# Letting a second group of heads start its recurrence halfway through the first

## The chip, the cores and the metric

The kernel runs on one core of a Trainium2 chip. The metric is the device time of one execution in microseconds (us), lower being better. Three runs of the kernel before took 1333.76, 1340.32 and 1342.75 us; the median is 1340.32 us. Five engines work side by side, each through its own list of instructions in order: PE (matrix products, with its weight loads shown apart as PEld), DVE (element-wise vector work), ACT (activations and copies), POOL (a second, slower vector engine) and SP (which here only issues DMA transfers). ACT issues DMA transfers too.

## The reference

A trunk of two layers on 512 tokens with 1024 features, in float32. Layer 0 is a spatial-gating MLP and layer 1 an RWKV-7 mixer; each is followed by a gated convolutional feed-forward block, and a last norm closes. The change lies in the RWKV-7 mixer. Its heart is a recurrence over time in 16 heads of 64 features:

```python
def step(state, inp):
    r_t, w_t, k_t, v_t, a_t, b_t = inp
    sa = jnp.einsum('bhvk,bhk->bhv', state, a_t)
    state = (state * w_t[:, :, None, :]
             + sa[..., None] * b_t[:, :, None, :]
             + v_t[..., None] * k_t[:, :, None, :])
    y_t = jnp.einsum('bhvk,bhk->bhv', state, r_t)
    return state, y_t
...
y = wkv7_scan(r_h, decay, k_h, v_h, -kk, kk * a_h)
...
y = (y + bonus.reshape(B, S, D)).astype(h.dtype)
return (y * g) @ w_o
```

Here `r`, `k` and `v` are dense projections of the token-shifted input, `g` is a low-rank gate, and the result `y` is normalised in each head before it is gated and multiplied by `w_o`.

## The kernel before

**The recurrence in chunks.** The 512 steps are cut into eight chunks of 64. Inside a chunk the recurrence is solved with products of 64x64 blocks; from chunk to chunk only the state goes on. What a chunk needs is prepared for all chunks beforehand and kept in DRAM: `std` (the factors that meet the state), `lpd` (lower-triangular blocks, one of which has to be inverted), `btd` and `vtd`. The heads are in pairs (eight pairs, 128 partitions each), and the pairs in two groups of four: group 0 is pairs 0 to 3, group 1 is pairs 4 to 7.

**The stages of the mixer.** `pairs()` makes, pair after pair, what goes to DRAM. `invert(g)` inverts the triangular blocks of group g by substitution: it reads them back (`li`, `lm`, lines L898 and L900), does 31 steps of two DVE instructions each (L910, L911), two transposes (L918, L919), then 32x32 products on PE (L930) with copies on ACT (L932), and stores the result (L915, L935). `scan(g)` is the recurrence of one group. `finish(g, b, y)` normalises the outputs of two chunks, and after every fourth chunk gates them. `projections()` makes keys and values with 128x512 dense products and is used as filler; it ends with the values of the last pairs. `project()` is the product with `w_o`, a filler as well, and may use a group's half only once that group is finished (`gated`).

**One chunk of the scan** is a chain of three links, each ending in a `yield`: the state meets the chunk's factors (PE L978 and L982) and DVE copies the product (L980); the inverted block is applied (PE L991), and DVE and ACT copy the halves (L992, L993); the new state is formed (PE L998, DVE L1001), while PE L1003 makes the chunk's output, which ACT copies (L1006). POOL scales the state meanwhile (L987). The transfers of chunk c+1, six on SP (L954 to L960: `st`, two `vu`, two `pt`, `cbt`), are issued at the start of chunk c.

**What sets the order.** The program is written by Python generators that take turns: `weave(main, side, fill, rate, lag, side_rate)` runs one step of `main`, then `side_rate` steps of `side` and `rate` steps of `fill`; the numbers stand in `RATES`. Around the change the order is:

```python
inv = invert(1)
next(inv)
gw = [gate_weights(g) for g in range(2)]
s0, s1 = scan(0), scan(1)
self.weave(s0, inv, fill, *RATES[2], ktiles=STEPS[2])
...
for k in range(KT):
    nc.sync.dma_start(self.h[k], r.hd[k])
fill = project()
self.weave(s1, None, fill, *RATES[3], ktiles=STEPS[3])
```

A scheduler then places the instructions in each engine's list. In the lists each DMA, from SP or from ACT, takes one of eight counters in turn and waits until the DMA that had this counter before has landed. So a transfer on SP can wait for one that ACT has not issued yet.

Of the kernel before, what the change touches and what calls it, by code (L numbers as in the profile page):

```python
# [2 lines left out]

# [18 lines left out]
KT = 8  # L22
# [7 lines left out]

RATES = ((1.9, 2), (1.9, 6, 2.2), (0.8, 2, 2), (0.6, 2))
WB = 4
FIRST0, WAIT, STEPS = 1, 4, (2, 2, 2, 2)
NKEY = 4
# [105 lines left out]
class Emit:  # L140
# [515 lines left out]
    def rwkv_main(self, r, ctx, gain):  # L656
        nc, tc, A = self.nc, self.tc, self.A
# [21 lines left out]
        ks, used, done, vdone = {}, set(), set(), set()  # L679
# [205 lines left out]

        def invert(g):

# [17 lines left out]
            for j in range(31):  # L905
                ni, nj = 31 - j, j + 1
                a = li[:, j, j + 1:32].unsqueeze(1).to_broadcast([P, nj, ni])
                b = tt[:, 0:nj, j].unsqueeze(2).to_broadcast([P, nj, ni])
                q = pr[:, 0:ni * nj].rearrange("p (c i) -> p c i", i=ni)
                V.tensor_tensor(q, a, b, ALU.mult)  # L910
                V.tensor_tensor(tt[:, 0:nj, j + 1:32], tt[:, 0:nj, j + 1:32], q, ALU.add)  # L911
                if j % 2 == 1:
                    yield
# [34 lines left out]
        chunks, outs, gated = {}, {}, set()  # L948
# [14 lines left out]
        def scan(g):  # L963
            ih = [(i, hd) for i in range(4) for hd in range(2)]
            y, late = None, iter(())
            for c in range(NCH):
                last = c == NCH - 1
                if c == 0:
                    load(g, 0)
# [44 lines left out]
        def finish(g, b, y):  # L1014
# [18 lines left out]
            if b % 2 == 1:  # L1033
                hs = slice((b - 1) * P, (b + 1) * P)
                yield
                if b == 1:
                    outs[g] = [tuple(self.xr.tile([P, T], F32R, tag=t, bufs=10, name=self.uid(t)) for t in ("mxh", "mxl"))
                               for _ in range(4)]
# [35 lines left out]
        def take(gen, n):  # L1074
            for _ in range(n):
                if next(gen, self) is self:
                    return
                yield

        def until(gen, end):  # L1080
            for _ in gen:
                yield
                if end():
                    return


        fill = projections()
# [11 lines left out]
        ep = ctx.enter_context(tc.tile_pool(name="scan", bufs=1))  # L1099
        inv = invert(1)  # L1100
        next(inv)
        gw = [gate_weights(g) for g in range(2)]
        s0, s1 = scan(0), scan(1)
        self.weave(s0, inv, fill, *RATES[2], ktiles=STEPS[2])
        for _ in inv:
# [5 lines left out]
        fill = project()  # L1111
        self.weave(s1, None, fill, *RATES[3], ktiles=STEPS[3])
        for _ in fill:
# [71 lines left out]
```

## Time and profile before

The profiled execution took 1336.87 us, 1335.0 us of which are its span.

| | us |
|---|---|
| median of 3 runs | 1340.32 |
| profiled execution, device time | 1336.87 |
| span of its profile | 1335.0 |
| PE busy in the span | 1269.7 |
| DVE busy | 842.3 |
| ACT busy | 605.6 |
| POOL busy | 140.8 |

The times in this text are counted from the span's start. The first feed-forward block and the mixer's low-rank part and projections lie ahead of 764 us; from there to 956 us lie the two scans, the rest of the fillers and the product with `w_o`; the second feed-forward block fills the rest. PE is counted busy while matmuls are under way, whose ends are modelled; a matmul that runs at half the clock is counted as busy for longer. In a list of instructions in order of time the columns are start, duration, engine, line, operation, output and inputs, count, and in brackets how long the engine was idle before it and what released it.

### The profile page before, as it was taken

Reading aid. Unit: us, or ns where it says so; the run is one execution under the profiler, and the core shown is the slowest. Engines: PE = TensorE matmul, PEld = TensorE weight load, DVE = VectorE, ACT = ScalarE, POOL = GpSimd, SP = SyncE. Lnnn points to the kernel's source line nnn. Section 1 sums busy time; section 2 is a strip of 40 time slices with the busy share of each in tenths; the row PEclk is TensorE's granted clock in tenths of the full one; section 3 lists DMA queues with packets and bytes.
Section 4 is the critical chain, followed back from the end, with each engine's and each line's share of the span. In section 5 each row is a group of like instructions: output and inputs, shape, how many; then the busy total and the mean of one; then the engine's idle time right before and its main releaser. Section 6 shows DMA issues by size and latency. Waiting matters only on the chain.

```text
span 1335.0 us, 19041 instructions
## 1 busy us (share of the span) xinstructions
PE 1269.7 (95%) x7490; PEld 1022.9 (77%) x7490; DVE 842.3 (63%) x1349; ACT 605.6 (45%) x1060; POOL 140.8 (11%) x152
## 2 busy tenths in 40 slices
PE   8999999999999999999989848798999999999996
PEld 6778888888888888777766636676888888888886
DVE  5565477777773335957979476556577777772223
ACT  5444354544443333667875424222454545452221
POOL 3100200000000001311210003232300000000001
PEclk9999999999999999999989869899999999999998
DMA  7232333323333333235866796962223333332322
GB/s 260 82 110 79 95 95 95 95 95 97 101 99 103 118 103 99 83 114 128 199 153 171 160 202 151 242 177 79 79 95 95 95 96 99 103 93 87 103 88 75
DMA packets 135786, 156.63 MB, mean 117 GB/s; under 512 B 64976, under 2 KB 100944, under 8 KB 135696
## 3 DMA queue, kind: packets, MB, share of 16 engines
q10 hardware_dynamic: 30688, 101.07, 24.9%
q1 hardware_dynamic: 105008, 54.34, 16.9%
q8 instruction: 59, 0.97, 0.3%
q14 instruction: 31, 0.25, 0.1%
HBM read 130.74 MB, written 24.64 MB: 116 GB/s over the span
## 4 chain that ended last, share of the span: by engine, by line
PE 79%; DVE 8%; ACT 2%; DMA 2%; issue 2%; POOL 1%; SPq 0%; ACTq 0%; DVEq 0%; POOLq 0%
PE mm L244 8%; PE mm L245 8%; PE mm L246 8%; PE e L244 5%; PE e L246 5%; PE e L245 5%; PE us L244 5%; PE us L246 5%; PE us L245 5%; PE aux L244 5%; PE aux L246 5%; PE aux L245 5%; DVE pr L910 1%; DVE tt L911 1%; PE us L978 1%
## 5 line engine op out<-in xcount | busy, mean ns | idle before, releaser
L205 ACT CAST wh<-w 128x512 fp32r<-128x512 f32 (+1 forms) x393 | 239.3, 613 | 441.5 <-PE mm L245 121.0
L206 DVE TENSOR_TENSOR wl<-w,wh 128x512 fp32r<-128x512 f32 (+1 forms) x385 | 267.0, 696 | 206.0 <-ACT wh L205 200.7
L244 PE MATMUL mm<-mxh,wh 128*128 128x512 f32 x424 | 175.1, 413 | 2.7 <-DVE rt L754 2.0
L245 PE MATMUL mm<-mxl,wh 128*128 128x512 f32 x424 | 169.8, 400 | 0.3 <-DVE mxl L1051 0.3
L246 PE MATMUL mm<-mxh,wl 128*128 128x512 f32 x424 | 168.3, 397 | 1.4 <-DVE wl L206 1.4
L271 POOL TENSOR_TENSOR ss<-ss,sq 128x512 f32<-128x512 f32 x30 | 40.4, 1347 | 777.5 <-issue 594.7
L244 PEld LDWEIGHTS mm<-mxh,wh 128*128 128x128 f32 x424 | 80.7, 191 | 25.3 <-issue 4.5
L246 PEld LDWEIGHTS mm<-mxh,wl 128*128 128x128 f32 x424 | 80.5, 190 | 19.2 <-DVE wl L206 2.1
L245 PEld LDWEIGHTS mm<-mxl,wh 128*128 128x128 f32 x424 | 80.7, 190 | 17.7 <-issue 1.4
L465 ACT ACTIVATE cv<-z,par 128x512 f32<-128x512 f32 x88 | 71.7, 817 | 30.4 <-DVE z L463 30.4
L244 PE MATMUL us<-mxh,wh 128*128 128x512 f32 (+1 forms) x216 | 84.5, 391 | 0.1
L244 PE MATMUL e<-mxh,wh 128*128 128x512 f32 x216 | 84.5, 391 | 0.0
L246 PE MATMUL us<-mxh,wl 128*128 128x512 f32 (+1 forms) x216 | 84.1, 389 | 0.0
L245 PE MATMUL us<-mxl,wh 128*128 128x512 f32 (+1 forms) x216 | 84.1, 389 | 0.0
L245 PE MATMUL e<-mxl,wh 128*128 128x512 f32 x216 | 84.0, 389 | 0.0
L246 PE MATMUL e<-mxh,wl 128*128 128x512 f32 x216 | 84.0, 389 | 0.0
L466 DVE SCALAR_TENSOR_TENSOR cv<-z,par,cv 128x512 f32<-128x512 f32 x88 | 66.0, 752 | 24.3 <-ACT cv L465 24.3
L244 PE MATMUL aux<-mxh,wh 128*128 128x512 f32 x208 | 81.2, 391 | 0.1
L246 PE MATMUL aux<-mxh,wl 128*128 128x512 f32 x208 | 81.1, 390 | 0.0
L245 PE MATMUL aux<-mxl,wh 128*128 128x512 f32 x208 | 80.9, 389 | 0.0
L467 DVE SCALAR_TENSOR_TENSOR cv<-z,par,cv 128x512 f32<-128x512 f32 x88 | 66.0, 752 | 2.9
L244 PEld LDWEIGHTS e<-mxh,wh 128*128 128x128 f32 x216 | 40.6, 188 | 8.8 <-issue 0.5
(1062 smaller groups left out, 2499.0 us busy)
## 6 DMA issues: line engine op xcount, KB each, us to landing
w<-in_wup ACTq DMA_DIRECT2D x88, 512.0 KB, 3.6
w<-in_wdn ACTq DMA_DIRECT2D x32, 512.0 KB, 3.6
st<-std SPq DMA_DIRECT2D x16, 512.0 KB, 6.4
w<-in_wdn ACTq DMA_DIRECT2D x16, 384.0 KB, 3.1
w<-in_wsu ACTq DMA_DIRECT2D x8, 512.0 KB, 3.9
w<-in_wso ACTq DMA_DIRECT2D x8, 512.0 KB, 3.6
w<-in_wk ACTq DMA_DIRECT2D x8, 512.0 KB, 4.3
std<-ar SPq DMA_DIRECT2D x16, 256.0 KB, 4.6
```

What stands on the lines that cost most here:

```text
L205: nc.scalar.copy(hi[r, :n], src)
L206: (lo_eng or nc.vector).tensor_tensor(lo[r, :n], src, hi[r, :n].bitcast(F32), ALU.subtract)
L244: mm(acc, wh, xh, start=first, stop=False)
L245: mm(acc, wh, xl, start=False, stop=False)
L246: mm(acc, wl, xh, start=False, stop=last)
L271: nc.gpsimd.tensor_tensor(self.ss, self.ss, self.sq, ALU.add)
L465: nc.scalar.activation(c, z[:, 2:], AF.Identity, scale=cw(2, i), bias=self.p("conv_b", l * 44 + i))
L466: nc.vector.scalar_tensor_tensor(c, z[:, 1:T + 1], cw(1, i), c, ALU.mult, ALU.add)
L467: nc.vector.scalar_tensor_tensor(c, z[:, 0:T], cw(0, i), c, ALU.mult, ALU.add)
L910: V.tensor_tensor(q, a, b, ALU.mult)
L911: V.tensor_tensor(tt[:, 0:nj, j + 1:32], tt[:, 0:nj, j + 1:32], q, ALU.add)
L978: nc.tensor.matmul(us[H[hd], 0, i, :], st[:, i, hd, 0:C], vu[:, i, hd, :], start=True, stop=True)
```

## The change

- The transfers of group 0's first chunk are issued ahead of those that `invert(1)` starts with.
- Three steps of the filler are put right behind these (`PREFILL`).
- The weights of the gates are fetched and split at the end of the filler, where before they were ahead of the scan.
- `invert(1)` gives way after every step of the substitution where it did after every second one, and gets 3.6 steps for each step of the scan where it got 2.
- After 12 steps (`LEAD`, four chunks) the first weave ends, and what is left of `invert(1)` and of the filler is written out. Then `turns(s0, s1)` alternates one step of group 0 with one of group 1. When group 0 is at its end, group 1 goes on alone.
- The filler's rates are 1.7 for 1.9 in the stage of the pairs, 1.8 for 0.8 in the first four chunks, 0.4 while the groups alternate, and 1 for 0.6 in the rest of group 1.

```diff
-RATES = ((1.9, 2), (1.9, 6, 2.2), (0.8, 2, 2), (0.6, 2))
+RATES = ((1.9, 2), (1.7, 6, 2.2), (1.8, 2, 3.6), (0.4, 2), (1, 2))
...
-        def invert(g):
+        def invert(g, every=2):
...
-                if j % 2 == 1:
+                if j % every == every - 1:
                     yield
...
-                if c == 0:
+                if c == 0 and (g, 0) not in chunks:
                     load(g, 0)
...
+        def turns(a, b):
+            for _ in a:
+                yield
+                if next(b, self) is not self:
+                    yield
...
-        inv = invert(1)
+        load(0, 0)
+        inv = invert(1, 1)
         next(inv)
-        gw = [gate_weights(g) for g in range(2)]
+        for _ in take(fill, PREFILL):
+            pass
+        gw = []
+
+        def gates():
+            for g in range(2):
+                with ExitStack() as after:
+                    for eng in (mybir.EngineType.DVE, mybir.EngineType.Activation):
+                        after.enter_context(tc.issue_after(self.last(eng)))
+                    gw.append(gate_weights(g))
+                yield
+
+        fill = chain(fill, gates())
         s0, s1 = scan(0), scan(1)
-        self.weave(s0, inv, fill, *RATES[2], ktiles=STEPS[2])
+        self.weave(take(s0, LEAD), inv, fill, *RATES[2], ktiles=STEPS[2])
...
         fill = project()
-        self.weave(s1, None, fill, *RATES[3], ktiles=STEPS[3])
+        self.weave(turns(s0, s1), None, fill, *RATES[3], ktiles=STEPS[3])
+        self.weave(s1, None, fill, *RATES[4], ktiles=STEPS[4])
```

No matmul is added or removed; what moves is their order. Lines of the changed kernel are higher by 1 up to the middle of `finish`, then by 2 and more.

SP's list at the end of the pairs, before (`lpd_4080` is group 0's block, `lpd_4081` group 1's; `st`, `vu`, `pt` and `cbt` are a chunk's transfers):

```order
L935 DMA lpd_4080<-lm_5797 32x32x32 x2
L744 DMA vtd<-vt_6589 128x8x64
L898 DMA li_6623<-lpd_4081 64x32x32 x2
L900 DMA lm_6624<-lpd_4081 32x32x32 x2
L954 DMA st_6655<-std 128x1024
L956 DMA vu_6658<-vtd 64x4x64
L957 DMA pt_6656<-lpd_4080 64x4x128
```

The same place now:

```order
L936 DMA lpd_4080<-lm_5797 32x32x32 x2
L955 DMA st_6594<-std 128x1024
L957 DMA vu_6597<-vtd 64x4x64
L958 DMA pt_6595<-lpd_4080 64x4x128
L957 DMA vu_6597<-vtd 64x4x64
L958 DMA pt_6595<-lpd_4080 64x4x128
L961 DMA cbt_6596<-btd 128x512
L899 DMA li_6606<-lpd_4081 64x32x32 x2
L901 DMA lm_6607<-lpd_4081 32x32x32 x2
```

The six transfers of group 0's chunk 0 went ahead of the four with which the substitution of group 1 begins; a store of values (`vtd`) that stood between moved elsewhere.

DVE's list where the substitution meets the scan, before: `wt_6688` is the first copy of chunk 0, and the 17th of the 31 substitution steps (`pr`, `tt`) surrounds it.

```order
L911 TENSOR_TENSOR tt_6625<-tt_6625,pr_6626 128x16x16
L910 TENSOR_TENSOR pr_6626<-li_6623,tt_6625 128x255
L980 COPY wt_6688<-us_6678 128x256
L911 TENSOR_TENSOR tt_6625<-tt_6625,pr_6626 128x17x15
L910 TENSOR_TENSOR pr_6626<-li_6623,tt_6625 128x252
```

The same step of the substitution now; `wt_6812` is the first copy of chunk 1.

```order
L912 TENSOR_TENSOR tt_6608<-tt_6608,pr_6609 128x16x16
L911 TENSOR_TENSOR pr_6609<-li_6606,tt_6608 128x255
L912 TENSOR_TENSOR tt_6608<-tt_6608,pr_6609 128x17x15
L981 COPY wt_6812<-us_6802 128x256
L911 TENSOR_TENSOR pr_6609<-li_6606,tt_6608 128x252
```

The whole of chunk 0 now stands ahead of the substitution's first step, and chunk 1 behind its 17th.

PE's list around chunk 4 of group 0 (`st_7013`), before; L246 is the end of a dense product, L738 and L752 belong to the values:

```order
L246 MATMUL mm_6960<-mxh_5659,wl_6759 128x512
L978 MATMUL us_7259<-vu_7016,st_7013 64x64 x8
L982 MATMUL e_7260<-vu_7016,st_7013 64x64 x8
L738 MATMUL mm_7287<-cst,v_7284 128x128 x4
L991 MATMUL us_7259<-wt_7269,pt_7014 64x64 x8
L752 MATMUL mm_7315<-rt_4089,wb_7313 128x512
L1003 MATMUL e_7260<-vu_7016,pt_7014 64x64
L998 MATMUL us_7259<-vu_7016,cbt_7015 64x64 x8
```

PE's list around the same chunk now (`st_7048` is chunk 4 of group 0, `st_7311` chunk 0 of group 1, `st_7278`'s partner `st_7275` chunk 5 of group 0):

```order
L931 MATMUL aux_7211<-li_7096,lm_6607 32x32 x32
L979 MATMUL us_7286<-vu_7051,st_7048 64x64 x8
L983 MATMUL e_7287<-vu_7051,st_7048 64x64 x8
L992 MATMUL us_7286<-wt_7296,pt_7049 64x64 x8
L1004 MATMUL e_7287<-vu_7051,pt_7049 64x64
L999 MATMUL us_7286<-vu_7051,cbt_7050 64x64 x8
L1004 MATMUL e_7287<-vu_7051,pt_7049 64x64 x7
L979 MATMUL us_7334<-vu_7314,st_7311 64x64
L983 MATMUL e_7335<-vu_7314,st_7311 64x64
L979 MATMUL us_7434<-vu_7278,st_7275 64x64 x8
```

The dense products ahead of chunk 4 and the values' products between its links are gone from this place, since the filler is used up earlier; PE goes from chunk 4 to the first product of group 1, and then to chunk 5 of group 0.

More of the change, by code (lines that the diff above doesn't have):

```diff
@@ L2 @@
 from contextlib import ExitStack
+from itertools import chain
 import numpy as np
@@ L29 @@
 C1 = -0.5 * math.exp(-0.5)
-RATES = ((1.9, 2), (1.9, 6, 2.2), (0.8, 2, 2), (0.6, 2))
+RATES = ((1.9, 2), (1.7, 6, 2.2), (1.8, 2, 3.6), (0.4, 2), (1, 2))
 WB = 4
-FIRST0, WAIT, STEPS = 1, 4, (2, 2, 2, 2)
+FIRST0, WAIT, PREFILL, LEAD, STEPS = 1, 4, 3, 12, (2, 2, 2, 2, 2)
 NKEY = 4
@@ L1036, in finish @@
                 if b == 1:
+                    assert KT - 1 in vdone
                     outs[g] = [tuple(self.xr.tile([P, T], F32R, tag=t, bufs=10, name=self.uid(t)) for t in ("mxh", "mxl"))
```

## Prediction

> **What bounds the kernel now.** I read the page first, then a table by stage, then the instructions of PE, SP and DVE in order of time from 764 to 956 us.
>
> ```profile
> PE 1269.7 (95%) x7490; PEld 1022.9 (77%) x7490; DVE 842.3 (63%) x1349; ACT 605.6 (45%) x1060; POOL 140.8 (11%) x152
> ```
>
> PE is the bound on average, so only time in which PE stands still or runs slowly can be won. The table by stage (length, then the busy time of PE, PEld, DVE, ACT, POOL, the granted clock, and the DMA engines' share and rate) says where that is:
>
> ```profile
> 764.00:784.00 20.00, 1.42 (x7) 0.77 (x6) 11.75 (x29) 6.45 (x11) 2.06 (x4) 0.62 1.07 220
> 784.00:827.00 43.00, 38.48 (x651) 29.38 (x651) 31.96 (x70) 15.86 (x35) 7.01 (x8) 0.90 0.66 152
> 827.00:864.00 37.00, 25.22 (x357) 21.30 (x356) 18.46 (x43) 10.62 (x27) 12.27 (x14) 0.82 1.02 236
> 864.00:921.00 57.00, 57.00 (x738) 41.59 (x737) 32.00 (x71) 16.14 (x39) 17.42 (x18) 1.00 0.59 155
> 921.00:956.00 35.00, 30.93 (x137) 24.85 (x136) 23.71 (x36) 16.64 (x31) 13.74 (x14) 0.95 0.20 61
> ```
>
> PE is idle for 18.6, 4.5, 11.8, 0 and 4.1 us in these five: 39 us of 192. The rows of PE that carry the argument:
>
> ```profile
> 783.66 0.37 PE L978 MATMUL us<-vu,st 128*64 128x64 f32 x2 [18.58 <-DMA vu<-vtd]
> 791.71 0.63 PE L244 MATMUL mm<-mxh,wh 128*128 128x512 f32 x1
> 792.13 0.63 PE L245 MATMUL mm<-mxl,wh 128*128 128x512 f32 x1
> 826.86 0.69 PE L978 MATMUL us<-vu,st 128*64 128x64 f32 x16
> 835.59 0.44 PE L978 MATMUL us<-vu,st 128*64 128x64 f32 x2 [3.14 <-DMA vu<-vtd]
> 844.96 0.33 PE L978 MATMUL us<-vu,st 128*64 128x64 f32 x2 [1.22 <-DVE vu L1001]
> 849.59 0.33 PE L978 MATMUL us<-vu,st 128*64 128x64 f32 x2
> 864.36 0.34 PE L978 MATMUL us<-vu,st 128*64 128x64 f32 x2
> 870.98 0.33 PE L978 MATMUL us<-vu,st 128*64 128x64 f32 x2
> 920.07 0.68 PE L1003 MATMUL e<-vu,pt 64*64 64x64 f32 x14
> 954.80 0.39 PE L245 MATMUL mm<-mxl,wh 128*128 128x512 f32 x1
> 955.03 0.39 PE L246 MATMUL mm<-mxh,wl 128*128 128x512 f32 x1
> ```
>
> Group 0 starts at 783.7 after a wait for its first transfers; its chunk 4 starts at 826.9, 5 at 835.6, 6 at 845.0, 7 at 849.6. Group 1 starts at 864.4, its last chunk ends at 920.7, and the dense products of its half are done at about 955.5. A dense product comes every 0.23 us at full clock (954.80 to 955.03) and every 0.42 at half clock, still eight us after the long gap (791.71 to 792.13).
>
> **The first transfers and the substitution.** SP's rows and two of DVE:
>
> ```profile
> 764.49 1.76 SPq L935 DMA_DIRECT2D lpd<-lm  x2
> 767.53 3.19 SPq L898 DMA_DIRECT2D li<-lpd  x2
> 770.81 3.86 SPq L900 DMA_DIRECT2D lm<-lpd  x2
> 774.84 2.82 SPq L954 DMA_DIRECT2D st<-std  x1
> 778.99 0.62 SPq L956 DMA_DIRECT2D vu<-vtd  x1
> 767.15 0.62 ACT L217 CAST gw<-w 32x512 fp32r<-32x512 f32 x1 [0.58 <-DMA btd<-bt]
> 776.70 0.19 DVE L910 TENSOR_TENSOR pr<-li,tt 128x31 f32<-128x31 f32 x1 [0.24 <-DMA li<-lpd]
> 789.17 0.42 DVE L980 COPY wt<-us 128x256 f32<-128x256 f32 x1
> 797.01 0.42 DVE L980 COPY wt<-us 128x256 f32<-128x256 f32 x1 [0.47 <-PE us L978]
> ```
>
> Now `li` and `lm` go first (767.5 to 774.7) and chunk 0 comes behind. With the order turned, `st` can go when the last pair's stores have landed, as the first `gw` did: 767.2. The second `vu` follows after `st` (0.5), `vu` (0.6) and `pt`, which waits for the block stored at 764.5 (I let it land by 769, an estimate of some 4 us from the two landing times quoted further below): issue at 769.8, and with the 5.5 us that it takes today (778.99 to 784.5) chunk 0 starts at about 774.5, **9 us sooner**. Of the stall of 18.6 us some 13 are covered or gone: 21 dense products more stand ahead of chunk 0 (33 where 12 were), at 0.23 each 4.8 us.
>
> The other side: `li` goes at 771.8 in place of 767.5, is usable 9.2 us later (767.53 to 776.70), and in DVE's list the substitution now stands behind the whole of chunk 0, which, at half clock with five dense products in between, takes from 774.5 to about 783.6. Its first step moves from 776.7 to some 784.3. Seventeen steps take 12.5 us (776.70 to 789.17), with one value's product 13.2: chunk 1's first copy comes at **797.5**, against 797.0 now. The 9 us are gone by then.
>
> **Up to chunk 4.** Today 37.7 us lie between the 17th step (789.2) and chunk 4 (826.9), with chunk 0's 7.8 (789.17 to 797.01) in it. Now chunk 0 is over: 29.9, so chunk 4 could start at 827.4. Three things speak for later: the gates' weights (four DVE instructions, two of 0.7 and two of up to 1.1: 3.5 us) come among DVE's steps here, where today they ran in the stall; ACT's casts of them stand ahead of its copies for chunk 2 and wait for their transfers; and its casts for `w_o` stand ahead of the copy for chunk 3.
>
> ```profile
> w<-in_g ACTq DMA_DIRECT2D x2, 256.0 KB, 3.4
> pt<-lpd SPq DMA_DIRECT2D x32, 128.0 KB, 5.6
> ```
>
> Two waits of 3.4 us, partly under DVE's steps: I take 4 us in all, chunk 4 at **831** (bounds 827, nothing of it, and 838, all of 3.5 and 6.8). Dense work is no cover any more here: 30 dense products are left where 48 were, and they are through during the substitution.
>
> **The hole before group 1.** Today the block's store, the seven reloads of `h` and the chunks' transfers run like this:
>
> ```profile
> 825.97 2.08 SPq L935 DMA_DIRECT2D lpd<-lm  x2
> 836.12 0.53 SPq L954 DMA_DIRECT2D st<-std  x1
> 840.22 0.38 SPq L954 DMA_DIRECT2D st<-std  x1
> 845.71 5.91 SPq L1110 DMA_DIRECT2D h<-hd  x7
> 851.71 0.38 SPq L954 DMA_DIRECT2D st<-std  x1
> 855.50 0.38 SPq L954 DMA_DIRECT2D st<-std  x1
> ```
>
> A chunk's six transfers take 4.1 and 3.8 us to issue. In the changed list the store (2.1, at 830.6, when ACT has copied the last of the blocks), `h` (5.9), chunk 5 of group 0 (4) and chunk 0 of group 1 follow each other; the first `vu` of the latter is issued at about 843 and lands 5 us later: both groups go on at **848**. Chunk 4 runs from 831 to 836 (4.6 from 844.96 to 849.59, without filler), so PE has a new hole of 12 us, with nothing to fill it.
>
> **Taking turns.** Eleven chunks remain: three of group 0, eight of group 1. The first two together I put at 9 us, as chunk 5 took today (835.59 to 844.96, at half clock behind a gap and with gate products). The next six have neither filler nor, most, gate products: between 4.6 (today without filler) and 6.6 (with, 864.36 to 870.98) I take 5.0, near the first, since their links fit between each other's and their transfers come at about 4 to 5 (1.18 MB each by the shapes in SP's list above, at the 236 GB/s of the third stage 5.0). That is 30, to 887. The last three carry two gatings and the filler again and are put at today's (920.7-864.4)/8 = 7.0 each: group 1 ends at **908**, 13 us before 920.7.
>
> **The end.** Today 110 dense products are left at group 1's end, now 150: 40 x 0.23 = 9.2 us more. Of today's 34.8 us PE is idle for 4.1 while the last norm runs, and at half clock behind it; now 30 products stand in that place. I take 6 off: 38 us, so the mixer ends at **946** where it ended at 955.5.
>
> **Sum:** -9.5 us. The second block is unchanged behind it. 1336.9 - 9.5 = 1327.4 against the profiled execution, which was 3.4 below the median: against the median 1330.8. I say 1330.
>
> **A rule of the skill against it.** After the gap of 18.6 us PE still worked at half clock eight us into its work, and there it had dense products. The turns have none, and a hole ahead of them. The Trainium skill, "TensorE: Matmul & The Clock Gate", Part 1 on the clock gate, says that an idle window of about 3.4 us halves the clock and about as much sustained work gives it back; its section on oscillation shows kernels whose waits keep it halved. By this the turns could run at half clock throughout (rival 2).
>
> **The rivals.**
>
> 1. *More is won (0.30).* The waits on ACT before chunk 4 are hidden: chunk 4 at 827, both groups on at 844; the six chunks at 4.6: 844 + 9 + 27.6 + 21 = 901.6, and 37 behind it, 938.6: -17, **1323** by the median. For it: DVE has steps to run meanwhile. Against: it is in order, and ACT too.
> 2. *Half clock through the turns (0.13).* Rows of the same products at the two clocks:
>
> ```profile
> 838.12 1.12 PE L1029 MATMUL aux<-cst,y 128*128 128x128 f32 x4
> 851.32 0.66 PE L1029 MATMUL aux<-cst,y 128*128 128x128 f32 x4
> 839.16 1.12 PE L991 MATMUL us<-wt,pt 64*64 64x64 f32 x16
> 851.90 0.68 PE L991 MATMUL us<-wt,pt 64*64 64x64 f32 x16
> ```
>
>    0.44 us more for one link's products, 1.2 to 1.3 for the three of a chunk; times the six: 7.5, so -2: **1338**. Against it: from 844.96 to 853 today PE ran such chunks at full clock without filler. It decides when gaps of 3 us and more stand between the links.
> 3. *The transfers on SP stop (0.10).* Today SP stood twice for transfers of `w_o` that ACT issues late:
>
> ```profile
> SPq L957 <- DMA w<-in_wo: 12.5, 2, 10.9
> ```
>
>    Each SP transfer waits for the one eight before it, and now also for buffers that two groups share. One stop of 10.9 before group 1 begins and another in the turns, uncovered since no filler is there: +21.8 - 9.5 = +12.3, **1353, slower**. In the list no transfer of ACT stands among those of the turns, which speaks against the second; four stand before chunk 4's end. It decides from 10 us of stops on.
> 4. *Nothing is interleaved (0.05).* Group 1's data come so late that group 0 ends alone: chunks 5 to 7 at 4.6 behind 846, then eight of 7.0 behind 860: 916, with 38: 954, **1339**.
>
> **The numbers.** The forecast has 0.42; its own range, from chunk 4 between 827 and 834 and the six chunks between 4.6 and 6, is 1324 to 1340. The range must also hold rival 1 with the hole smaller by some 5 us (transfers landing sooner) and half of rival 3: 1313 to 1347. One per cent is 13.4 us, about what three runs that differ by 9 can tell. Faster by more: rival 1 and a fifth of the forecast, 0.38. Slower by more: rival 3 lies at that bound, and most of it is counted, 0.08. Within: 0.54.
>
> **What would show it.** Right: chunk 0 at about 774.5 and a substitution beginning near 784; chunk 1's copy at 797; a PE gap of some 12 us between chunk 4 and group 1's first product, ended by a transfer; chunks every 5 us behind it; the last chunk of group 1 near 908. Wrong: a substitution that starts before 780, chunk 4 before 826 or behind 838, a clock of 0.5 through the turns, or SP waiting for `w_o` there.

## The result and the profile after

The kernel after took 1351.02 us in the median of eight runs (1344.6 to 1356.57), the kernel before on the same chip 1339.58 us (eight runs, 1333.76 to 1343.64). The ratio is 1.0085, with a 95% interval of 1.0057 to 1.0114: 11.4 us slower. The prediction had 1330, a range of 1313 to 1347, and 0.08 for slower by over 1%. Direction and range were wrong. That the change stays within 1% had 0.54, but for a gain; that it came out within 1% on the other side is luck and bears out no step.

The profiled execution took 1352.91 us with a span of 1351.1; that of before had 1336.87 and 1335.0. So these two traces differ by 16 us, and the sums below are made against the 16.

The page's line of engine totals, after:

```profile
PE 1279.7 (95%) x7490; PEld 1037.4 (77%) x7490; DVE 840.1 (62%) x1349; ACT 605.4 (45%) x1060; POOL 141.7 (10%) x152
```

PE has the same 7490 matmuls and is busy for 10.0 us longer (1279.7 against 1269.7): the same work at a lower clock. The other 6 us are time in which PE stands still.

The table by stage, with the stages cut at the same events in both kernels: from the store of group 0's inverted halves (`lpd<-tt`) to chunk 0, to chunk 4, to group 1's first product, to its last, to the last dense product of the mixer. Columns: window, length, busy time of PE, PEld, DVE, ACT and POOL, granted clock, DMA share, GB/s. Before:

```profile
754.46:783.66 29.20, 10.62 (x232) 8.55 (x232) 12.14 (x29) 10.72 (x20) 3.17 (x6) 0.73 0.98 196
783.66:826.86 43.20, 38.68 (x649) 29.57 (x648) 32.27 (x71) 15.71 (x35) 7.01 (x8) 0.89 0.66 153
826.86:864.36 37.50, 25.72 (x359) 21.57 (x358) 18.46 (x43) 10.95 (x27) 12.27 (x14) 0.82 1.02 236
864.36:920.70 56.34, 56.34 (x736) 41.18 (x735) 32.00 (x71) 15.72 (x37) 17.42 (x18) 1.00 0.59 155
920.70:960.02 39.32, 35.25 (x155) 28.44 (x155) 26.75 (x39) 18.78 (x35) 14.27 (x14) 0.96 0.21 62
```

After:

```profile
756.58:780.06 23.48, 19.95 (x196) 15.79 (x195) 2.68 (x4) 8.14 (x18) 2.96 (x6) 0.76 0.75 144
780.06:838.61 58.55, 41.33 (x632) 32.75 (x632) 40.24 (x96) 21.53 (x46) 8.09 (x9) 0.77 0.79 164
838.61:857.34 18.73, 5.65 (x83) 4.90 (x81) 3.14 (x7) 1.68 (x4) 6.02 (x10) 0.50 1.00 260
857.34:932.99 75.65, 66.94 (x963) 55.45 (x963) 43.67 (x102) 20.56 (x51) 18.97 (x20) 0.85 0.59 151
932.99:976.04 43.05, 42.34 (x195) 34.83 (x195) 28.89 (x43) 20.60 (x38) 17.02 (x16) 1.00 0.27 82
```

The stall ahead of chunk 0 is gone, as it should be (29.20 us with 10.62 of work, now 23.48 with 19.95). The stage behind it is 15 us longer, with no more products for PE (632 for 649) but 8 us more work for DVE (40.24 for 32.27), since more of the substitution lies in it. The stage from chunk 4 to group 1 is half as long, the one of group 1, now the turns, is longer by 19 us, and the end by 3.7. The clock is lower in the second, third and fourth stage. Busy time times one minus the clock, summed over the rows, is 13 us before and 27 after: that much of PE's busy time, by this estimate, is the half clock.

### The profile page after: what moved, and what is told of

It is laid out like the page before. It is cut to its first block, busy times and chain, and to the rows that moved or that the text cites. A ratio compares the mean times of both kernels' runs of the same rounds, so it can differ in the third digit from the quotient of the medians.

```text
span 1351.1 us, 19031 instructions
## 1 busy us (share of the span) xinstructions
PE 1279.7 (95%) x7490; PEld 1037.4 (77%) x7490; DVE 840.1 (62%) x1349; ACT 605.4 (45%) x1060; POOL 141.7 (10%) x152
## 5 line engine op out<-in xcount | busy, mean ns | idle before, releaser
L246 PE MATMUL mm<-mxl,wh 128*128 128x512 f32 x424 | 168.2, 397 | 0.0
L246 PEld LDWEIGHTS mm<-mxl,wh 128*128 128x128 f32 x424 | 80.6, 190 | 16.1 <-issue 0.9
L246 PE MATMUL us<-mxl,wh 128*128 128x512 f32 (+1 forms) x216 | 84.1, 389 | 0.0
L246 PE MATMUL e<-mxl,wh 128*128 128x512 f32 x216 | 84.1, 389 | 0.0
L246 PE MATMUL aux<-mxl,wh 128*128 128x512 f32 x208 | 80.9, 389 | 0.0
```

The costliest lines, as they stand in the source:

```text
L246: mm(acc, wh, xl, start=False, stop=False)
```

## The experiments

The ideas under test were: the turns themselves cost what they bring (T); the order of the first loads delays the substitution of group 1 more than it helps (L); the reload of `h` stands in the hole (H); the half clock makes chunks without filler long (C). The numbers run in the order in which the runs were made. Each ratio is to the kernel before on the same chip.

A common measure in them is the distance from the store of group 0's inverted halves to: the store of group 0's whole block (`lpd<-lm`), chunk 0's first product, the substitution's first step, the store of group 1's block, and the last product of group 1. In us, each from one trace, so that a few us are not sure: between chunk 0 and the store of group 1's inverted halves e8 and e11 have the same 326 products of PE, in 31.3 us at a clock of 0.86 and in 35.5 us at 0.74.

| kernel | block 0 | chunk 0 | substitution | block 1 | group 1's end | ratio, 95% |
|---|---|---|---|---|---|---|
| before | 10.0 | 29.2 | 22.2 | 71.5 | 166.3 | 1 |
| after | 15.5 | 23.5 | 33.5 | 82.8 | 176.4 | 1.0085 [1.0057, 1.0114] |
| e1: after without turns | 15.8 | 24.5 | 34.3 | 81.8 | 176.3 | 1.0078 [1.0062, 1.0094] |
| e8: before with turns | 9.7 | 29.4 | 22.0 | 71.3 | 165.1 | 1.0005 [0.9989, 1.0021] |
| e9: before, chunk 0 loaded first | 9.1 | 19.1 | 35.3 | 81.6 | 175.8 | 1.0053 [1.0033, 1.0073] |
| e13: after, old order, early gates | 11.7 | 29.7 | 30.1 | 78.2 | 170.2 | 1.0052 [1.0031, 1.0072] |
| e12: before, turns one chunk later, `h` later | 9.7 | 26.0 | 21.9 | 72.0 | 162.7 | 0.9943 [0.9926, 0.9960] |

### The turns: e1, e8 and e6

e1 undoes the turns alone:

```diff
-self.weave(take(s0, LEAD), inv, fill, *RATES[2], ktiles=STEPS[2])
+self.weave(s0, inv, fill, *RATES[2], ktiles=STEPS[2])
...
-self.weave(turns(s0, s1), None, fill, *RATES[3], ktiles=STEPS[3])
-self.weave(s1, None, fill, *RATES[4], ktiles=STEPS[4])
+self.weave(s1, None, fill, 0.6, 2, ktiles=STEPS[4])
```

> The changed kernel without the turns: group 0 goes through all eight chunks, then h is reloaded, then group 1 runs alone with 0.6 steps of filler. All else as in the changed kernel (loads, substitution, gates' weights, rates). PE's list is the same up to the end of chunk 4. Theory T (the turns themselves take more than they give): chunk 4 again near 838.6; group 1's first product comes at about 866 in place of 857, but its eight chunks take 56 us (as before the change) in place of 75.7, so group 1 ends near 922 in place of 933 and the tail is as long as before the change (39): the kernel takes 1337 to 1341 us. Theory A (the time is lost ahead of the turns, which are neutral): 1347 us or more.

Measured: 1348.15 us, 1.0078 [1.0062, 1.0094]. The loss is still there without turns. In its trace group 1 ends 176.3 us behind the store of the halves, with turns 176.4. T falls as the cause of the loss, and so does the prediction's gain: with the turns the kernel is no faster.

e8 is the other side, the kernel before with the turns and nothing else:

```diff
-RATES = ((1.9, 2), (1.9, 6, 2.2), (0.8, 2, 2), (0.6, 2))
+RATES = ((1.9, 2), (1.9, 6, 2.2), (0.8, 2, 2), (0.4, 2), (1, 2))
-FIRST0, WAIT, STEPS = 1, 4, (2, 2, 2, 2)
+FIRST0, WAIT, LEAD, STEPS = 1, 4, 12, (2, 2, 2, 2, 2)
...
-self.weave(s0, inv, fill, *RATES[2], ktiles=STEPS[2])
+self.weave(take(s0, LEAD), inv, fill, *RATES[2], ktiles=STEPS[2])
...
-self.weave(s1, None, fill, *RATES[3], ktiles=STEPS[3])
+self.weave(turns(s0, s1), None, fill, *RATES[3], ktiles=STEPS[3])
+self.weave(s1, None, fill, *RATES[4], ktiles=STEPS[4])
```

> The kernel before with the turns alone: after chunk 3 of group 0 both groups take turns, with 0.4 steps of filler there and 1 in the rest of group 1; loads, substitution, gates' weights and filler up to there as before the change. Theory N (the turns are neutral, as the kernel without them was only 1 us faster than the changed one; the loss lies ahead of chunk 4): the ratio to the kernel before is 0.998 to 1.004. Theory T (the turns lose where the stage ahead of them is in order): 1.005 or more. As predicted for the turns in the first place, they would win some 10 us: 0.992.

Measured: 1340.02 us, 1.0005 [0.9989, 1.0021]. Its stages from the hole on, columns as above:

```profile
831.50:846.00 14.50, 0.14 (x4) 0.03 (x1) 1.17 (x3) 0.74 (x2) 3.85 (x7) 0.52 1.07 289
846.00:918.15 72.15, 62.94 (x963) 52.15 (x963) 43.58 (x102) 20.56 (x51) 18.97 (x20) 0.91 0.65 157
918.15:961.21 43.06, 42.35 (x195) 34.82 (x196) 28.89 (x43) 20.60 (x38) 17.01 (x16) 1.00 0.26 81
```

Group 1 begins at 846.0 where it began at 864.4. Measured from the store of the halves, so that the start of this trace counts for nothing, that is 17 us sooner; its end is 1.2 us sooner, and the mixer's end 2.6 us later, since 40 more dense products follow. The turns give all of their lead back, though here nothing ahead of them was changed: the eleven chunks take 72.15 us, where the prediction had 60.

e6 asks whether the half clock is why. It adds to the kernel after dense products that nobody reads, and leaves nothing out; the trace has 88 of them, 34 in the hole and 54 in the turns:

```diff
+def spare(n):
+    a = self.acc("mm")
+    for _ in range(n):
+        nc.tensor.matmul(a, gw[0][0][:, 0:P], r.sg[0], start=True, stop=True)
...
+with tc.issue_after(self.last(mybir.EngineType.PE)):
+    spare(30)
+self.weave(both, None, spares(), 1, 2, ktiles=STEPS[3])
-self.weave(turns(s0, s1), None, fill, *RATES[3], ktiles=STEPS[3])
```

> The changed kernel with 86 more dense products whose result nobody reads: 34 in the hole between chunk 4 and group 1's first product, 52 spread over the turns and the chunk behind them; project() then begins only behind the turns, where it could start anyway. Nothing is left out. At full clock they are 19.8 us of PE work. Theory C (PE's half clock, from gaps without filler, is what makes the turns long): the hole's 34 cost nothing, the clock in the turns stays at 1, and the turns take no longer although 12 us of products are added: 1345 to 1355 us. Rival (the turns are long because of PE's own products and the waits between links, the clock matters little): the turns become longer by most of the 12 us, 1360 us or more.

Measured: 1354.5 us, 1.0109 [1.0093, 1.0124], about 3 us more than after by the ratios. The window of the turns in it:

```profile
860.00:934.60 74.60, 73.73 (x1011) 57.07 (x1012) 41.69 (x102) 20.58 (x51) 18.66 (x20) 0.96 0.58 150
```

There are 48 more products in it (54 added, six of `w_o` fewer), 11 us at full clock, and the window is still 1.05 us shorter than 75.65: the clock is 0.96 where it was 0.85. So the half clock does lengthen the turns, and C holds. Yet PE is then busy for 73.73 of 74.60, the added products included: with 11 us taken off, 63 us of its own work are left by this estimate, more than the 60 of the prediction. As a whole the kernel got slower, so the clock was not won back for nothing.

### The reload of h: e4, e11 and e12

e4 issues the seven reloads of `h` three steps later, behind the loads of group 1's first chunk, in the kernel after; e11 does the same in e8:

```diff
-for k in range(KT):
-    nc.sync.dma_start(self.h[k], r.hd[k])
-fill = project()
+def reload():
+    yield
+    yield
+    yield
+    for k in range(KT):
+        nc.sync.dma_start(self.h[k], r.hd[k])
+    yield
+fill = chain(reload(), project())
```

> The changed kernel with the reload of h moved behind the first transfers of group 1 and some chunks into the turns. Theory H (the hole of 12.5 us in front of group 1 is SP's list: h's 4.5 us stand ahead of group 1's first chunk): the hole becomes 8 us, the turns start at 853, and the kernel takes 1346 to 1348 us. Rival (the hole is set by the landing of the inverted blocks and the rate of the transfers, and h takes its share later): the hole stays above 10 us or the turns give it back, 1350 to 1352 us.

Measured: 1342.99 us, 1.0055 [1.0034, 1.0077]. Group 1's first product in the two traces, after:

```profile
857.34 0.45 PE L979 MATMUL us<-vu,st 128*64 128x64 f32 x2 [12.49 <-DMA vu<-vtd]
```

and e4:

```profile
854.26 0.45 PE L979 MATMUL us<-vu,st 128*64 128x64 f32 x2 [7.04 <-DMA vu<-vtd]
```

The hole is 5.4 us shorter, and the time by the ratios 4 us. The intervals of the two ratios overlap, so it is the row, and e11 with a like gain, that bear H out.

> The kernel before with the turns, and the reload of h some chunks into them. Theory H: as in the changed kernel (1.0085 to 1.0055) this takes 4 us out of the hole in front of group 1 (14.4 us with the turns alone), so 0.996 to 0.999 of the kernel before. Rival (the time is given back to transfers later): 1.000 to 1.002.

Measured: 1335.23 us, 0.9974 [0.9958, 0.9990], 4 us less than e8 again (the intervals just touch). In the one trace of each the gain can't be seen, since e11's met the lower clock named above ahead of the hole. e12 moves the beginning of the turns one chunk further back in e11, from 12 steps to 15:

```diff
-FIRST0, WAIT, LEAD, STEPS = 1, 4, 12, (2, 2, 2, 2, 2)
+FIRST0, WAIT, LEAD, STEPS = 1, 4, 15, (2, 2, 2, 2, 2)
```

> As the kernel before with turns and late h, but the turns set in one chunk later (15 steps in place of 12), so chunk 5 of group 0 lies ahead of group 1's first product in PE's list and its transfers, and chunk 6's, ahead of group 1's. If the hole in front of group 1 is idle time that chunk 5 can fill, 0.992 to 0.997 of the kernel before. If group 1's transfers come later by the ones put ahead (4 to 5 us a chunk), nothing is won: 0.998 to 1.002.

Measured: 1331.21 us, 0.9943 [0.9926, 0.9960]: faster than both kernels. Its hole and its turns:

```profile
834.54:851.09 16.55, 7.89 (x101) 6.91 (x101) 6.14 (x15) 3.15 (x8) 4.17 (x8) 0.72 0.98 191
851.09:917.32 66.23, 59.58 (x881) 48.75 (x881) 38.07 (x91) 18.52 (x45) 18.66 (x19) 0.91 0.76 188
```

One more chunk of group 0 runs while group 1's transfers are under way. The idle gap ahead of group 1's first product is 5.9 us in this trace, where it is 9.9 in e11.

### The order of the first loads: e9 and e10

e9 is the kernel before with chunk 0's loads ahead of the substitution's, and nothing else:

```diff
+load(0, 0)
 inv = invert(1)
```

> The kernel before with one part of the change: the transfers of group 0's chunk 0 are issued ahead of the substitution's li and lm. No turns, gates' weights early, all rates as before. Theory L (this order is what the change loses by: the substitution of group 1, which nothing but DVE can do and on which group 1 waits, starts behind chunk 0): the substitution begins 8 us or more later after the store of the inverted halves than before the change (22 us there), the second block's store too, and the ratio to the kernel before is 1.005 to 1.008. Rival (the loss comes from the late end of the pair stage and the late gates' weights, which this kernel does not have): 0.997 to 1.003.

Measured: 1346.62 us, 1.0053 [1.0033, 1.0073]: 7 us slower. Two rows of DVE, the second of them the substitution's first step:

```profile
787.52 0.69 DVE L206 TENSOR_TENSOR wl<-w,wh 128x512 fp32r<-128x512 f32 x1 [4.32 <-ACT wh L205]
...
788.85 0.18 DVE L910 TENSOR_TENSOR pr<-li,tt 128x31 f32<-128x31 f32 x1
```

Chunk 0 is 10 us sooner, the substitution 13 us later (35.3 us behind the halves for 22.2), because it now stands behind a whole chunk and a filler's split of weights; group 1's block is stored 10 us later, and group 1 ends 9.5 us later. L holds, for the kernel before.

e10 puts the old order back into the kernel after:

```diff
-load(0, 0)
 inv = invert(1, 1)
 next(inv)
+load(0, 0)
```

> The changed kernel with li and lm ahead of chunk 0's transfers again; late gates' weights, rates, three filler steps ahead and the turns stay. Theory L: the substitution starts 26 to 28 us behind the store of the inverted halves in place of 33.5, the second block is stored near 75 us in place of 82.8, and the ratio to the kernel before is 0.999 to 1.003 in place of 1.0085. Rival (late pair end, late gates' weights, filler spent early): 1.006 to 1.010.

Measured: 1350.47 us, 1.0087 [1.0054, 1.0119], no gain. Here the substitution begins 25.0 us behind the halves, and its transposes are done at 817.2. What was won is lost on SP, where the store of the new halves has its place behind a chunk's transfers:

```profile
828.13 0.33 SPq L961 DMA_DIRECT2D cbt<-btd  x1
828.57 3.98 SPq L916 DMA_DIRECT2D lpd<-tt  x2
```

SP's longest waits in that stretch are for ACT's copies of the values (20.1 us in three), and another names the gates' weights, which ACT issues (waiting engine and line, what it waited for: us in total, times, longest):

```profile
SPq L961 <- DMA w<-in_g: 3.8, 1, 3.8
```

So two chains end at the same store, one over DVE and one over SP, and mending the first alone gains nothing. L alone is not the whole loss. Whether mending both does is what e13 asks, below.

### The gates' weights: e2 and e14

e2 puts the gates' weights ahead of the scan again in the kernel after:

```diff
+gw = [gate_weights(g) for g in range(2)]
...
-gw = []
...
-fill = chain(fill, gates())
```

> The changed kernel with the gates' weights fetched and split ahead of the scan again, as before the change. Theory G (the casts of these weights wait for their transfer on ACT and hold up the copies of chunks 2 and 3): ACT's wait of 2.9 us and DVE's of 1.9 us in front of them go, chunk 4 comes at 834 to 835 in place of 838.6, and the kernel takes about 1347 us. Rival (the substitution on DVE sets the pace there and hides them): chunk 4 stays at 837 to 839 and the time at 1350 to 1352 us.

Measured: 1357.18 us, 1.0143 [1.0125, 1.0161], worse than either of the two expectations. SP's two longest waits from 760 to 800 us:

```profile
SPq L961 <- DMA w<-in_wv: 7.9, 1, 7.9
SPq L958 <- DMA w<-in_wo: 5.9, 1, 5.9
```

The fillers now begin early, so their weights, issued by ACT, stand between the transfers of chunks 0 and 1; SP waits for them through the shared counters, and the substitution begins 38.9 us behind the halves.

e14 is the kernel before with the gates' weights behind the first six steps of the scan:

```diff
-gw = [gate_weights(g) for g in range(2)]
+gw = []
 s0, s1 = scan(0), scan(1)
+self.weave(take(s0, 6), inv, fill, *RATES[2], ktiles=STEPS[2])
+for g in range(2):
+    with ExitStack() as after:
+        for eng in (mybir.EngineType.DVE, mybir.EngineType.Activation):
+            after.enter_context(tc.issue_after(self.last(eng)))
+        gw.append(gate_weights(g))
```

> The kernel before with the gates' weights fetched and split after six steps of the scan (two chunks) in place of ahead of it; nothing else changed, no turns. Theory M: the late gates' weights alone hold the substitution's end: the second block is stored 78 us or more behind the store of the inverted halves (71.5 before the change), and the ratio is 1.004 to 1.010. Rival: 0.998 to 1.002.

Measured: 1341.39 us, 1.0015 [0.9998, 1.0032], hardly to be told from nothing, and group 1's block is stored 74.9 us behind the halves, not 78 or more: theory M fails here, and the late gates alone cost little. But it shows where the late store of group 0's block comes from. Its rows of DVE:

```profile
761.20 0.69 DVE L206 TENSOR_TENSOR wl<-w,wh 128x512 fp32r<-128x512 f32 x1 [11.58 <-PE mm L246]
764.28 0.69 DVE L206 TENSOR_TENSOR wl<-w,wh 128x512 fp32r<-128x512 f32 x1 [2.39 <-ACT wh L205]
764.89 0.68 DVE L843 TENSOR_TENSOR lq<-us,cst 128x512 f32<-128x512 f32 x1
```

and of SP's waits:

```profile
SPq L844 <- DVE lq L843: 6.9, 1, 6.9
```

With the gates' weights away, the splits of the next fillers' weights (`wl`) stand on DVE ahead of the last pair's `lq`, and wait for PE and ACT; SP waits 6.9 us for `lq`, and the stores behind it wait with it. Group 0's block is stored 16.1 us behind the halves, 10.0 before. The block is as late, 15.2 to 16.1 us, in the traces of all nine kernels with late gates (after, e1, e3 to e7, e10 and e14), and at 9.1 to 11.7 us in all seven with early ones.

### Fillers and rates: e3, e5, e7 and e13

e3 puts the filler's rate in the stage of the pairs back:

```diff
-RATES = ((1.9, 2), (1.7, 6, 2.2), (1.8, 2, 3.6), (0.4, 2), (1, 2))
+RATES = ((1.9, 2), (1.9, 6, 2.2), (1.8, 2, 3.6), (0.4, 2), (1, 2))
```

> The changed kernel with the filler's rate in the stage of the pairs back at 1.9 (1.7 in the change). Theory P (the last pair's stores are late because of this rate: with fewer filler steps ahead, casts of filler weights stand in front of the last copies on ACT, while PE works at half clock): the store of group 0's block goes out near 764.5 in place of 772.1, everything behind comes 7 us sooner, 1343 to 1345 us. Rival (the store is late for another reason, such as the order in which the scheduler places the last copies): it stays behind 770 and the time stays at 1349 to 1352 us.

Measured: 1348.75 us, 1.0083 [1.0061, 1.0104]. The block is as late (16.1). The rate is not it.

e5 pins the fillers of the scan behind the last `lq` and the last `bt` of the pairs:

```diff
+ends[0] = self.last(mybir.EngineType.DVE)
...
+ends[1] = self.last(mybir.EngineType.Activation)
...
+with ExitStack() as after:
+    for i in ends.values():
+        after.enter_context(tc.issue_after(i))
+    self.weave(take(s0, LEAD), inv, fill, *RATES[2], ktiles=STEPS[2])
-self.weave(take(s0, LEAD), inv, fill, *RATES[2], ktiles=STEPS[2])
```

> The changed kernel with one thing pinned: the first filler weights that belong to the scan's stage may not be cast (ACT) or split (DVE) before the last pair's last masked product (lq) and its last copy (bt) stand in the lists. On PE and SP the lists stay as they are. Theory Q (the pair stage ends late because DVE's split of filler weights stands ahead of the last lq and waits 14.6 us for a cast on ACT, which waits for PE): from the store of the inverted halves (line of L916) to the store of group 0's block some 11 us in place of 15.5, the whole kernel 4 to 5 us shorter than the changed one, 1345 to 1347 us. Rival (the half clock of PE there holds the pair stage, whatever DVE's order): 15 us remain and the time stays near 1350 us.

Measured: 1351.92 us, 1.0093 [1.0075, 1.0112]. The last `lq` starts at 755.1 and no longer waits, but SP does:

```profile
760.78 0.57 SPq L846 DMA_DIRECT2D lpd<-lq  x1
767.21 0.57 SPq L847 DMA_DIRECT2D std<-lq  x1
769.98 1.49 SPq L938 DMA_DIRECT2D lpd<-lm  x2
```

The store at 767.21 follows `w<-in_wv`, which ACT issued at 762.82 and whose landing releases it. The block stays at 15.9: one wait took the place of another.

e7 puts the fillers of the first four chunks back to what they were:

```diff
-RATES = ((1.9, 2), (1.7, 6, 2.2), (1.8, 2, 3.6), (0.4, 2), (1, 2))
+RATES = ((1.9, 2), (1.7, 6, 2.2), (0.8, 2, 2), (0.4, 2), (1, 2))
-FIRST0, WAIT, PREFILL, LEAD, STEPS = 1, 4, 3, 12, (2, 2, 2, 2, 2)
+FIRST0, WAIT, PREFILL, LEAD, STEPS = 1, 4, 0, 12, (2, 2, 2, 2, 2)
...
-inv = invert(1, 1)
+inv = invert(1, 2)
```

> The changed kernel with the filler held back for the first four chunks: no filler steps ahead of chunk 0, 0.8 steps of filler and 2 of the substitution for each link (as before the change), and the substitution gives way after every second step again; the loads' order, the late gates' weights and the turns stay. Theory C (filler spent ahead of chunk 1 leaves PE with gaps and at half clock in chunks 2 to 4): PE loses less to half clock between chunk 0 and chunk 4, chunk 4 comes 48 to 53 us behind chunk 0 in place of 58.5, and the kernel takes 1343 to 1347 us. Rival (the links wait for DVE and ACT there, filler only gets in their way): 58 us remain, 1350 us or more.

Measured: 1364.5 us, 1.0189 [1.0167, 1.0210], the worst of all. The block of group 1 is stored sooner (79.7 us behind the halves), but what is left of the filler, and with it the gates' weights, falls into the hole:

```profile
867.76 0.45 PE L979 MATMUL us<-vu,st 128*64 128x64 f32 x2 [22.13 <-DMA vu<-vtd]
```

SP's waits for transfers that ACT issued, 832 to 875 us:

```profile
SPq L1132 <- DMA w<-in_g: 6.5, 1, 6.5
SPq L958 <- DMA w<-in_wo: 5.6, 2, 2.8
SPq L961 <- DMA w<-in_wo: 3.9, 1, 3.9
```

Together 16 us in the stretch around the hole. The faster filler is thus not a mistake of the change taken by itself: with the gates' weights behind it, it has to be through when the turns begin after four chunks. With these weights early, in e8, the slow filler does no harm there.

e13 is the kernel after with both the old order of loads and the early gates; what is left of the change are the turns, the rates, `PREFILL` and the finer substitution:

```diff
-load(0, 0)
 inv = invert(1, 1)
 next(inv)
+gw = [gate_weights(g) for g in range(2)]
+load(0, 0)
```

> The changed kernel with two parts undone at once: li and lm go ahead of chunk 0's transfers again, and the gates' weights are fetched and split ahead of the scan again. Turns, rates, three filler steps ahead stay. Theory M (two delays of about the same length end at the store of the second block: the substitution that starts late, and the gates' weights that hold ACT, DVE and SP just when its halves and products are copied and stored; each alone costs the 8 to 11 us, so undoing one changed nothing): 0.998 to 1.003 of the kernel before, the second block's store 70 to 75 us behind the store of the inverted halves (82.8 in the changed kernel). Rival (it is the filler, spent early, and the half clock behind it): 1.006 or more.

Measured: 1344.78 us, 1.0052 [1.0031, 1.0072]. Since the turns are worth 1.0005 (e8), the fillers' share is 0.0047, about 6 us, and the intervals of the two runs don't overlap. Theory M expected at most 1.003, and group 1's block at 70 to 75 us; it is stored at 78.2. So two hidden delays, undone together, account for some 0.0033 of the 0.0085, and even that is not clear of noise, since the intervals of after and e13 overlap. SP's waits for ACT's transfers, 760 to 850 us:

```profile
SPq L745 <- DMA w<-in_wo: 6.8, 1, 6.8
SPq L957 <- DMA w<-in_wv: 6.5, 1, 6.5
SPq L961 <- DMA w<-in_wo: 3.2, 1, 3.2
```

The substitution begins 30.1 us behind the halves though its loads go out as early as before: DVE has the splits of the gates' and of the greedy fillers' weights ahead of it.

## Why the prediction was wrong, point by point

Two steps of the prediction failed. The turns were put at 60 us; they took 75.65, and 72.15 in e8, where nothing ahead of them was changed. And group 0's block was taken to be stored where it was, at 764.5; it was stored at 772.05. Landmarks in us from the start of the span:

| | before | predicted | after |
|---|---|---|---|
| group 0's block stored | 764.5 | 764.5 | 772.1 |
| chunk 0 | 783.7 | 774.5 | 780.1 |
| substitution's first step | 776.7 | 784.3 | 790.1 |
| chunk 1's first copy | 797.0 | 797.5 | 805.0 |
| chunk 4 | 826.9 | 831 | 838.6 |
| group 1's first product | 864.4 | 848 | 857.3 |
| group 1's last product | 920.7 | 908 | 933.0 |

**The first transfers.** The forecast kept the block's store at 764.5. SP's rows, after:

```profile
772.05 1.47 SPq L936 DMA_DIRECT2D lpd<-lm  x2
774.43 0.34 SPq L955 DMA_DIRECT2D st<-std  x1
778.08 3.75 SPq L899 DMA_DIRECT2D li<-lpd  x2
```

and the wait ahead of them:

```profile
SPq L845 <- DVE lq L844: 5.0, 1, 5.0
```

The block is stored 7.6 us later. 2.1 of these are there already at the store of the halves; 5.4 arise behind it, and e14 puts them on the late gates, a part that the prediction counted only with 4 us of waits ahead of chunk 4. With 7.6 added, chunk 1's copy would come at 805.1 and chunk 4 at 838.6; measured were 805.0 and 838.6. That agreement is in part luck: chunk 0 (782.1 by this, 780.1 measured) and the substitution (791.9, 790.1) came 2 us sooner, and no run has the 4 us of waits on ACT by themselves. The forecast had looked at what the moved transfers wait for, and not at what moves up into the place they leave.

**The substitution.** DVE's first step, after:

```profile
789.45 0.69 DVE L755 TENSOR_TENSOR rt<-mm,v 128x512 f32<-128x512 f32 x1 [2.22 <-PE mm L753]
790.06 0.18 DVE L911 TENSOR_TENSOR pr<-li,tt 128x31 f32<-128x31 f32 x1
```

That the 9 us are gone by chunk 1 was right. But the delay of the substitution goes on to group 1's block, whose store is 82.8 us behind the halves' where it was 71.5. The prediction had it at 830.6 for 826.0, a loss that the turns would make good. e9 shows that this exchange alone costs 7 us.

**The hole** was right: 12 us predicted, 12.49 measured, ended by the transfer that was named; chunk 4 to group 1 took 18.7 for 17.

**The turns** are the largest error, 75.65 us for 60. They start at 857.34 (row above); the rows of PE at the beginning of the six chunks, in them and behind them, after:

```profile
865.77 0.33 PE L979 MATMUL us<-vu,st 128*64 128x64 f32 x2
...
891.86 0.33 PE L979 MATMUL us<-vu,st 128*64 128x64 f32 x2
...
901.58 0.53 PE L979 MATMUL us<-vu,st 128*64 128x64 f32 x4
...
906.82 0.33 PE L979 MATMUL us<-vu,st 128*64 128x64 f32 x2
...
919.02 0.33 PE L979 MATMUL us<-vu,st 128*64 128x64 f32 x2
```

The first two chunks took 8.4 (9 predicted). The six that were put at 5.0 each took 41.05 in place of 30, the last three 26.2 in place of 21:

```profile
865.77:906.82 41.05, 32.88 (x524) 27.77 (x523) 21.91 (x56) 10.99 (x28) 12.10 (x14) 0.79 0.81 209
906.82:932.99 26.17, 25.63 (x308) 20.43 (x307) 18.83 (x40) 8.54 (x21) 6.61 (x7) 1.00 0.08 23
```

In the six PE stands still for 8.2 us, and by the estimate used above (busy time times one minus the clock) loses 6.9 to the half clock; 26 us of its work are left. e6 has the same six chunks at a clock of 1.00 with 46 added products in them: PE is busy there for 40.3 us, which without these (0.23 each) leaves 30. So 5.0 a chunk was hardly more than PE's own work, 26 to 30 us by these two estimates; the forecast left nothing for the half clock and for waits. In the last three chunks PE's work alone is 25.6 us at full clock, more than the 21.

Where the time lies in the six: four of them are near the forecast, together 22 us, 5.5 each, the step from 875.06 to 891.86 at a clock of 0.74. The prediction had most of the six without work beside the recurrence; two have it: the first (865.77 to 875.06) has 16 products of group 0's gates in it, the fifth (891.86 to 901.58, 9.7 us, clock 0.79) eight products of the norms, ahead of the last four of which PE stood 2.0 us for DVE. Behind 906.82 the gating of both groups meets in one chunk of 12.2 us, with 13 dense products of `w_o`. So the mis-sized term is that of the turns: the gates and norms of two groups do not shrink when their chunks alternate, and half clock and waits come on top.

**The end** took 3.7 us more, predicted were 3.2 (38 for 34.8). The prediction read 955.5 as the end of the dense products at the edge of its rows; they ran to 960.0, with 134 behind the last chunk where it counted 110. After there are 174, so the difference of 40 was right, and nothing of the sum hangs on it.

**The sum:** -9.5 predicted, +7.6 for the block's late store, +1.7 in the hole, +15.7 in the turns, +0.5 at the end: +16.0, which is what the two traces differ by. This adds up places, not causes: in e14 the block is as late, and the time hardly changes.

**The rivals.** Rival 2, half clock through the turns, came true in part: 0.85 there and 0.50 in the hole ahead, with e6 to show that it costs something. Its price for the six chunks, 7.5 us, is close to the 6.9 estimated above; its time of 1338 fell short because the waits, the work of the last three chunks and the late block were not in it. Rival 3, SP waiting for transfers of ACT, is seen in e2, e5, e7, e10 and e13 (3 to 8 us a wait); what these waits cost by themselves was not measured, and in the kernel after only 3.8 us of them appear ahead of chunk 4. Rivals 1 and 4 did not come: chunk 4 was not hidden, and the groups did interleave.

**Where the loss is.** By single parts: the turns 1.0005, the late gates 1.0015, the order of loads 1.0053, the fillers with their rates 1.0047 (e13 over e8). The sum would be 1.012, the whole is 1.0085: that several delays end at the same store, that of group 1's block, and hide one another would fit this, and e10 and e5, but e13 bears it out at most in part. What stays open, beside this, is which of the fillers' parts (three steps ahead, 1.8 for 0.8, 3.6 steps of the finer substitution, 1.7 for 1.9) makes the 0.0047; only the last was tried alone, in the full change, and makes no difference there, and the other three were undone together only in e7, where the late gates spoil the result.

The granted clock goes with most of the loss. Over the 72 runs of the kernel before that were made beside the experiments, a run takes some 8 us more for each 0.01 of clock that it has less (correlation -0.91). The eight runs of the kernel after have 0.962 on average, those 72 have 0.974, which by this line is 9 of the 11.4 us. This does not say which comes first: the hole of 12.49 us is itself followed by a clock of 0.65 through the first two chunks of the turns, and e6 raised the clock without a gain.

## What to carry to other kernels

An earlier start of a chain is worth only what its last link gains: look in the profile for the work that both chains share, and let it stand in the sum at its full length, with the waits and the half clock that it has in the rows. When transfers or weights move away from a place, ask what the scheduler puts there in their stead, and what then waits for it. And where two delays seem to end at one event, undo them together as well as one at a time: here undoing one gained nothing (1.0087 and 1.0143), and undoing both still left more than half of the loss (1.0052).

## What the runs showed of the hardware

The clock behind a short gap of PE did not follow one rule. The rows are window, length, PE's busy time, granted clock, DMA share and GB/s; PE's list up to here is the same in the first two kernels. Before:

```profile
743.00:745.00 2.00, 0.35 (x1) 0.99 0.00 0
745.00:754.50 9.50, 9.15 (x83) 0.50 0.73 175
754.50:764.00 9.50, 9.50 (x230) 0.96 0.82 147
```

e8, the same place:

```profile
742.00:744.00 2.00, 0.21 (x1) 1.00 0.00 0
744.00:754.00 10.00, 9.80 (x234) 1.00 0.79 186
```

After:

```profile
744.00:750.40 6.40, 3.98 (x17) 1.00 0.09 18
750.40:767.00 16.60, 16.60 (x292) 0.51 0.79 156
```

A gap of 2.0 us was followed by some 9 us at half clock in one trace, and by none in the other. In the kernel after, two gaps of 1.1 and 1.3 us were followed by 16.6 us at half clock in which PE did not pause once; e1 shows the same (from 748 to 765 us, clock 0.50). The Trainium skill, "TensorE: Matmul & The Clock Gate", Part 1, has the clock halved by an idle window of about 3.4 us and given back by as much sustained work. These traces differ on both counts: shorter gaps were enough, and 16.6 us of sustained work were not. The page's caveats, that the events of the gate in a trace have been unreliable and that the gate has been seen stuck at a quarter of the clock for 50 us and more, do not settle it. The matmuls themselves are slower, so it isn't only the record: from the gap on the same list got through 83 of them in 9.5 us before and through 234 in 10 us in e8.
